# A two-layer hybrid block (gated feed-forward, S5 and sparse attention): the wide GpSimd arithmetic of the S5 preparation and of the rotary products moved to VectorE and ScalarE

## The chip, the cores and the metric

One Trainium2 chip, one NeuronCore of it. The metric is the device time of one execution in microseconds. In the profile PE is TensorE's matmul side and PEld its weight load, DVE is VectorE, ACT is ScalarE, POOL is GpSimd, SP is the SyncE queue that issues the weight transfers.

## What is computed

Input `x` is 256 tokens by 1024, float32. Two layers each do this:

```
x = x + 0.5 * swiglu(rms_norm(x, norm_ffn1), ffn1_wi, ffn1_wo)      # 1024 -> 2*2816 -> 1024
h = rms_norm(x, norm_mix)
u, q, k/v for three attention branches, gates = split(h @ w_in)     # 1024 -> 3864
y_a = s5_branch(u, lambda, dt, b, c, d, w_glu)                      # diagonal state space, 32 groups x 64 states
y_b = nsa_branch(q, k, v, gates, norms, ...) @ nsa_w_up             # rms norm + rotary on q and k, three attentions
x = x + (sigmoid(gate_a) * y_a + sigmoid(gate_b) * y_b) @ w_out
x = x + 0.5 * swiglu(rms_norm(x, norm_ffn2), ffn2_wi, ffn2_wo)
```

The S5 branch needs matrices that depend on parameters alone: powers of a complex decay per state, the scaled input matrix times these powers, the output matrix times these powers, and a short convolution kernel over four lags. The kernel calls this the preparation and does it once per layer. Rotary embedding multiplies each head by a cosine table and its swapped halves by a sine table, and adds the two.

## The kernel before

**Weights and matmuls.** Every matmul is computed as three float32r passes: a weight tile of 128x1024 is loaded by SP into `raw` (four buffers) and split into a rounded part `whi` by ACT and a remainder `wlo` by DVE. Gain-scaled weights (`wi`, `w_in`) are split by lines 156 and 157, in two pieces of 128x512 for each tile; the others (`wo`) by line 318 in one piece of 128x1024. There are four `whi` and four `wlo` buffers, so a tile can be split only when PE is done with the tile four places earlier. Lines 350 to 352 are the three passes.

**A feed-forward network** runs over 11 chunks of 256 hidden columns. In each chunk PE does the gate and up products of this chunk (four weight tiles, 48 matmuls into `gu`), then the output products of the chunk before (two tiles, 24 matmuls into `ya` and `yb`, one for each half of the tokens). ACT applies silu (line 450), DVE multiplies (line 451, result `w1k`), PE transposes the result (line 434), and ACT and DVE split it (line 318, `w1k`). After the last chunk `finish` runs the output products of that chunk, adds `ya` and `yb` to `x` on DVE (line 360), transposes the new `x` on PE (line 344) and splits it into `hh` (ACT) and `hl` (DVE): the stationary operand of every matmul of the next stage. I call this stretch the end of the first feed-forward network.

**The preparation of the S5 parameters** is a generator that runs beside the first feed-forward network of each layer: `prep` calls `s5_load`, `s5_scalars`, `s5_tables` and `s5_mats`. Each `yield` gives back a cost; `next`, which hands out the next weight tile, pulls from the generator until a credit of 0.75 is used up. What is left when the network has been written is written out in one piece by `drain_bg`, before the mixing stage. `cmul` is a complex product: four products and two sums. In `s5_mats` it is called three times for 128x256 operands and four times for 128x512 operands with the four products on POOL (`M=G`), which cost nothing against the credit.

**The rotary products** are in `normrope` (keys, and one compressed key) and `normrope_q`: the cosine product on DVE, the two swapped halves with the sine on POOL, the sum on DVE.

**The order of the instructions** on each engine is set when the kernel is built: a scheduler simulates the program and lists each engine's instructions by simulated time, with the written order as priority. At run time each engine takes its list strictly in order.

Of the kernel before, what the change touches and what calls it, by code (L numbers as in the profile page):

```python
# [74 lines left out]
class Model:  # L75
# [445 lines left out]
            nc.gpsimd.dma_start(P['c'][:, i], bass.AP(tensor=t, offset=o, ap=[[64, 128], [8192, 4], [1, 64]]))  # L521
        k.P = P

    def cmul(k, o, a, b, tmp, cost, M=None, conj=False):

        V = k.nc.vector
        M = M or V
        c = cost if M is V else 0.0
        t0, t1 = tmp(), tmp()
        M.tensor_mul(t0, a[0], b[0])  # L530
        yield c
        M.tensor_mul(t1, a[1], b[1])
        yield c
        (V.tensor_add if conj else V.tensor_sub)(o[0], t0, t1)
        yield cost
        t2, t3 = tmp(), tmp()
        M.tensor_mul(t2, a[0], b[1])
        yield c
        M.tensor_mul(t3, a[1], b[0])
        yield c  # L540
        (V.tensor_sub if conj else V.tensor_add)(o[1], t2, t3)
        yield cost

# [127 lines left out]
    def s5_tables(k):  # L671

        nc, P = k.nc, k.P
        V, G = nc.vector, nc.gpsimd
        cs = k.sb([128, 16, 64], "r4", k.opt['n4'])
        sn = k.sb([128, 16, 64], "r4", k.opt['n4'])
        de = k.sb([128, 16, 64], "r4", k.opt['n4'])
        P['cs'], P['sn'], P['de'] = cs, sn, de
        G.memset(cs[:, :, 0:1], 1.0)
        G.memset(sn[:, :, 0:1], 0.0)  # L680
        k.gcopy(de, P['m4'][:, :, None].to_broadcast([128, 16, 64]))
        G.memset(de[:, :, 0:1], 0.0)
        R = k.sb([128, 14, 16], "w1k", k.opt['n1'])
        cur = P['u4']
        m = 1
        i = 0
        while m < 64:
            W = [k.sb([128, 16, m], "w2k", k.opt['n2']) for _ in range(2)]
            br = cur[0][:, :, None].to_broadcast([128, 16, m])
            bi = cur[1][:, :, None].to_broadcast([128, 16, m])  # L690
            c0, s0 = cs[:, :, 0:m], sn[:, :, 0:m]
            c1, s1 = cs[:, :, m:2 * m], sn[:, :, m:2 * m]
            cost = 0.07 + 0.0167 * m
            V.tensor_mul(W[0], c0, br)
            yield cost
            V.tensor_mul(W[1], s0, bi)
            yield cost
            V.tensor_sub(c1, W[0], W[1])
            yield cost
            V.tensor_mul(W[0], s0, br)  # L700
            yield cost
            V.tensor_mul(W[1], c0, bi)
            yield cost
            V.tensor_add(s1, W[0], W[1])
            yield cost
            m *= 2
            if m < 64:
                nx = (R[:, 2 * i], R[:, 2 * i + 1])
                t0, t1 = R[:, 12], R[:, 13]
                V.tensor_mul(t0, cur[0], cur[0])  # L710
                V.tensor_mul(t1, cur[1], cur[1])
                V.tensor_sub(nx[0], t0, t1)
                V.tensor_mul(t0, cur[0], cur[1])
                V.tensor_scalar(nx[1], t0, 2.0, None, op0=ALU.mult)
                yield 0.4
                cur = nx
                i += 1

    def s5_mats(k):
        nc, P = k.nc, k.P  # L720
        V, G, S = nc.vector, nc.gpsimd, nc.scalar
        r4 = lambda: k.sb([128, 1024], "r4", k.opt['n4'])
        r8 = lambda: k.sb([128, 2048], "r8", k.opt['n8'])
        b, pw, f = P['b'], P['pw'], P['f']
        bc = lambda s, n=16: s[:, :, None].to_broadcast([128, 16, n])
        tmp1 = lambda: k.sb([128, 16, 16], "w1k", k.opt['n1'])

        X = [r4().rearrange("p (a t c) -> p a t c", a=16, t=4) for _ in range(2)]
        bb = (X[0][:, :, 3], X[1][:, :, 3])
        yield from k.cmul(bb, (bc(f[0]), bc(f[1])), (b[:, 0], b[:, 1]), tmp1, 0.34)  # L730
        for m in (1, 2, 3):
            yield from k.cmul((X[0][:, :, 3 - m], X[1][:, :, 3 - m]), (bc(pw[m][0]), bc(pw[m][1])), bb, tmp1, 0.34, G)

        CT = []
        for i in range(2):
            cd = k.sb([128, 4, 2, 64], "w2k", k.opt['n2'])
            V.tensor_mul(cd, P['c'][:, i, :, None].to_broadcast([128, 4, 2, 64]), k.C('m2')[:, None, :, None].to_broadcast([128, 4, 2, 64]))
            bk = k.bank((128, 4, 128))
            for q in range(4):
                nc.tensor.transpose(bk[:, q], cd[:, q].rearrange("p a b -> p (a b)"), k.id)  # L740
            ct = k.sb([128, 16, 32], "w2k", k.opt['n2'])
            S.copy(ct.rearrange("p (q r) c -> p q (r c)", q=4), bk)
            CT.append(ct)
            yield 0.6
        nci = k.sb([128, 16, 32], "w2k", k.opt['n2'])
        V.tensor_scalar(nci, CT[1], -1.0, None, op0=ALU.mult)
        yield 0.34

        P['G'], XX = [], []
        for i in range(2):  # L750
            xx = r8().rearrange("p (a g c) -> p a g c", a=64, g=2)
            for g in range(2):
                G.tensor_scalar(xx[:, :, g], X[i].rearrange("p a t c -> p (a t) c"), k.C('m64')[:, g:g + 1], 0.0,
                                op0=ALU.mult, op1=ALU.add)
            xx = xx.rearrange("p (a t) g c -> p a (t g c)", a=16)
            XX.append(xx)
            gm = r8().rearrange("p (a b) -> p a b", a=16)
            for h in range(4):
                bk = k.bank((128, 4, 128))
                for q in range(4):  # L760
                    nc.tensor.transpose(bk[:, q], xx[:, h * 4 + q], k.id)
                S.copy(gm[:, h * 4:h * 4 + 4], bk)
                yield 0.5
            P['G'].append(gm)

        bk = k.bank((128, 4, 64))
        for q in range(4):
            for i, c in enumerate((CT[0], nci)):
                for r in range(4):
                    p = 4 * q + r  # L770
                    nc.tensor.matmul(bk[r * 32:(r + 1) * 32, q], c[:, p], X[i][:, p].rearrange("p t c -> p (t c)"),
                                     start=(q == 0 and i == 0), stop=(i == 1), skip_group_check=True)
        lt = k.sb([128, 16, 2, 16], "w2k", k.opt['n2'])
        V.tensor_mul(lt, bk.rearrange("p q (t c) -> p (q t) c", t=4)[:, :, None].to_broadcast([128, 16, 2, 16]),
                     k.C('m2')[:, None, :, None].to_broadcast([128, 16, 2, 16]))
        yield 0.6
        lt = lt.rearrange("p (q t) g c -> p q (t g c)", q=4)
        bk = k.bank((128, 4, 128))
        for q in range(4):
            nc.tensor.transpose(bk[:, q], lt[:, q], k.id)  # L780
        bk = bk.rearrange("p q (r c) -> p (q r) c", r=4)
        lag = k.sb([128, 16, 32], "w2k", k.opt['n2'])
        S.copy(lag, bk)
        yield 0.5
        dg = k.sb([128, 16, 32], "w2k", k.opt['n2'])
        V.tensor_mul(dg[96:128], k.C('i32')[96:128, None, :].to_broadcast([32, 16, 32]),
                     P['d'][96:128, :, None].to_broadcast([32, 16, 32]))
        yield 0.6
        V.tensor_add(lag[96:128], lag[96:128], dg[96:128])
        yield 0.6  # L790
        ks = r8().rearrange("p (a s c) -> p a s c", a=16, s=4)
        G.memset(ks, 0.0)
        for t in range(4):
            for s in range(t, 4):
                r = 3 - s + t
                k.gcopy(ks[t * 32:(t + 1) * 32, :, s], lag[r * 32:(r + 1) * 32])
        P['K'] = ks.rearrange("p a s c -> p a (s c)")

        cr, ci = (r8().rearrange("p (a s c) -> p a s c", a=16, s=4) for _ in range(2))
        tmp2 = lambda: k.sb([128, 16, 32], "w2k", k.opt['n2'])  # L800
        for s in range(4):
            a = (bc(pw[s + 1][0], 32), bc(pw[s + 1][1], 32))
            yield from k.cmul((cr[:, :, s], ci[:, :, s]), a, (CT[0], nci), tmp2, 0.6, G, True)
        P['C'] = [m.rearrange("p a s c -> p a (s c)") for m in (cr, ci)]


# [128 lines left out]
    def normrope(k, src, nh, cg, sg, out, tabs):  # L935
# [14 lines left out]
        for h in range(2):  # L950
            a, b = slice(h * 32, h * 32 + 32), slice((1 - h) * 32, (1 - h) * 32 + 32)
            T, Q = tabs(t2), tabs(qn)
            ix = (slice(None),) * (len(T.shape) - 1)
            G.tensor_mul(T[ix + (a,)], Q[ix + (b,)], sg[ix + (a,)])
        V.tensor_add(out, tabs(t1), tabs(t2))

    def kv_evac(k, t, kp, ps):
# [41 lines left out]
    def normrope_q(k, src, cg, sg, out):  # L999
# [11 lines left out]
        V.tensor_mul(t1, qn, cg)  # L1011
        for h in range(2):
            a, b = slice(h * 32, h * 32 + 32), slice((1 - h) * 32, (1 - h) * 32 + 32)
            G.tensor_mul(t2[:, :, a], qn[:, :, b], sg[:, :, a])
        for g in range(2):
            V.tensor_add(out[:, g], t1[:, g * 4:g * 4 + 4], t2[:, g * 4:g * 4 + 4])

# [355 lines left out]
```

## Time and profile before

| | us |
|---|---|
| median of three runs | 1189.49 (1189.47 to 1189.8) |
| the profiled execution | 1189.75 |
| its span, first to last instruction | 1187.7 |
| PE busy | 1157.4 |
| DVE busy | 840.5 |
| ACT busy | 674.7 |
| POOL busy | 232.2 |

The time outside the span is 2.05 us. PE is busy for 97% of the span, so there are about 30 us in which it has nothing to do; of these 7.35 us lie in the first 25 us and 4.1 us behind its last matmul. DVE is busy for 71% of the span on average, and for over 90% in the stretches in which POOL computes.

### The profile page before, as it was taken

The numbers are of one execution on the slowest core, as the hardware profiler recorded it, in microseconds if no ns is written. First come the engines' busy times: TensorE is split into PE (matmuls) and PEld (weight loads), VectorE is DVE, ScalarE is ACT, GpSimd is POOL, SyncE is SP. The second block draws the span as 40 slices with busy tenths as digits, with TensorE's granted clock in tenths as the row PEclk, the third lists the DMA queues.
The fourth block names the chain that finished last, engine by engine and source line by source line (L and its number), as shares of the span: only waits on it lengthen the run. The fifth ranks groups of instructions, "written<-read, shape, count | busy, mean of one in ns | idle before, by whom it ended". The sixth has DMA issues, their size and how long they took to land.

```text
span 1187.7 us, 18769 instructions
## 1 busy us (share of the span) xinstructions
PE 1157.4 (97%) x6710; PEld 944.1 (79%) x6710; DVE 840.5 (71%) x1494; ACT 674.7 (57%) x1176; POOL 232.2 (20%) x284
## 2 busy tenths in 40 slices
PE   7999999999999999999999999999999999999998
PEld 6888777877877888888888887778778778888886
DVE  5797979587976765555567987886878756655554
ACT  6655554755775565555566555546557646655552
POOL 3001644035032000000030044711441310000000
PEclk9999999999999999999999999999999999999999
DMA  7756555365442565655565656445635435656652
GB/s 236 221 182 194 154 157 186 103 184 168 143 142 92 168 213 185 194 182 186 185 193 173 197 165 183 138 156 154 196 108 170 132 105 161 214 181 192 189 183 89
DMA packets 150077, 200.46 MB, mean 169 GB/s; under 512 B 9952, under 2 KB 120832, under 8 KB 149984
## 3 DMA queue, kind: packets, MB, share of 16 engines
q1 hardware_dynamic: 148848, 197.46, 53.8%
q0 software_dynamic: 1136, 1.82, 0.9%
q8 instruction: 52, 0.85, 0.3%
q14 instruction: 41, 0.34, 0.1%
HBM read 198.18 MB, written 1.05 MB: 168 GB/s over the span
## 4 chain that ended last, share of the span: by engine, by line
PE 89%; POOL 3%; DVE 3%; ACT 2%; issue 2%; DMA 1%; SPq 0%; DVEq 0%; ACTq 0%
PE gu L352 19%; PE gu L350 19%; PE gu L351 19%; PE ya L352 4%; PE yb L350 4%; PE ya L350 4%; PE yb L352 4%; PE yb L351 4%; PE ya L351 4%; POOL r L480 2%; PE tr L434 2%; PE yb L1178 1%; DVE wlo L157 1%; PE tr L344 1%; PE tr L1167 1%
## 5 line engine op out<-in xcount | busy, mean ns | idle before, releaser
L157 DVE SCALAR_TENSOR_TENSOR wlo<-raw,gcol,whi 128x512 fp32r<-128x512 f32 (+2 forms) x480 | 359.0, 786 | 111.0 <-ACT whi L156 108.5
L156 ACT ACTIVATE whi<-raw,gcol 128x512 fp32r<-128x512 f32 (+2 forms) x480 | 316.2, 710 | 193.8 <-PE gu L351 91.0
L350 PE MATMUL gu<-whi,hh 128*128 128x512 f32 (+2 forms) x960 | 378.7, 395 | 0.4 <-ACT whi L156 0.4
L352 PE MATMUL gu<-wlo,hh 128*128 128x512 f32 (+2 forms) x960 | 375.4, 396 | 2.5 <-DVE wlo L157 2.5
L351 PE MATMUL gu<-whi,hl 128*128 128x512 f32 (+2 forms) x960 | 375.3, 391 | 0.0
L318 DVE TENSOR_TENSOR wlo<-raw,whi 128x1024 fp32r<-128x1024 f32 x128 | 161.0, 1260 | 102.0 <-ACT whi L318 99.3
L352 PEld LDWEIGHTS gu<-wlo,hh 128*128 128x128 f32 x960 | 180.8, 189 | 38.6 <-DVE wlo L157 2.8
L318 ACT CAST whi<-raw 128x1024 fp32r<-128x1024 f32 x128 | 134.5, 1053 | 133.3 <-PE gu L351 114.8
L351 PEld LDWEIGHTS gu<-whi,hl 128*128 128x128 f32 x960 | 181.2, 189 | 35.7
L350 PEld LDWEIGHTS gu<-whi,hh 128*128 128x128 f32 x960 | 181.3, 189 | 34.7 <-ACT whi L156 0.6
L325 POOL TENSOR_SCALAR rs<-ss 128x1 f32<-128x1 f32 (+3 forms) x22 | 7.2, 328 | 379.4 <-ACT w2k L332 352.6
L351 PE MATMUL yb<-whi,w1k 128*128 128x512 f32 x176 | 71.5, 406 | 0.7 <-DVE w1k L318 0.7
L352 PE MATMUL yb<-wlo,w1k 128*128 128x512 f32 x176 | 69.1, 393 | 0.0
L350 PE MATMUL yb<-whi,w1k 128*128 128x512 f32 x176 | 69.0, 395 | 0.0
L351 PE MATMUL ya<-whi,w1k 128*128 128x512 f32 x176 | 68.8, 391 | 0.0
L352 PE MATMUL ya<-wlo,w1k 128*128 128x512 f32 x176 | 68.7, 390 | 0.0
L350 PE MATMUL ya<-whi,w1k 128*128 128x512 f32 x176 | 68.2, 393 | 0.0
L318 ACT CAST w1k<-tr 128x256 fp32r<-128x256 f32 x88 | 32.5, 369 | 46.1 <-PE tr L434 46.1
L1157 POOL TENSOR_SCALAR w2k<-w2k,sm 128x128 f32<-128x128 f32 (+1 forms) x64 | 38.9, 629 | 99.8 <-ACT w2k L1141 62.8
L451 DVE SCALAR_TENSOR_TENSOR w1k<-gu,rs,w1k 128x256 f32<-128x256 f32 x88 | 42.0, 479 | 20.3 <-ACT w1k L450 20.2
L450 ACT ACTIVATE w1k<-gu,rs 128x256 f32<-128x256 f32 x88 | 40.9, 468 | 22.7 <-PE gu L352 17.8
L318 DVE TENSOR_TENSOR w1k<-tr,w1k 128x256 fp32r<-128x256 f32 x88 | 36.7, 419 | 10.3 <-ACT w1k L318 10.2
(307 smaller groups left out, 1474.7 us busy)
## 6 DMA issues: line engine op xcount, KB each, us to landing
raw<-in_ffn_wi_dram SPq DMA_DIRECT2D x352, 256.0 KB, 3.3
raw<-in_ffn_wo_dram SPq DMA_DIRECT2D x88, 512.0 KB, 3.6
raw<-in_w_in_dram SPq DMA_DIRECT2D x48, 512.0 KB, 4.4
raw<-in_ssm_w_glu_dram SPq DMA_DIRECT2D x32, 256.0 KB, 3.4
raw<-in_w_out_dram SPq DMA_DIRECT2D x16, 512.0 KB, 3.2
raw<-in_cmp_w_dram SPq DMA_DIRECT2D x8, 512.0 KB, 4.6
raw<-in_nsa_w_up_dram SPq DMA_DIRECT2D x16, 256.0 KB, 3.9
raw<-in_w_in_dram SPq DMA_DIRECT2D x8, 408.0 KB, 4.1
```

The source lines that it names most:

```text
L156: k.hi_ins[i] = k.nc.scalar.activation(hi[:, s], r[:, s], AF.Copy, scale=c)
L157: k.nc.vector.scalar_tensor_tensor(lo[:, s], r[:, s], c, hi[:, s].bitcast(F32), op0=ALU.mult, op1=ALU.subtract)
L318: return k.nc.scalar.copy(hi, src), k.nc.vector.tensor_sub(lo, src, hi.bitcast(F32))
L344: m = k.nc.tensor.transpose(b[:, i], src[:, i * 128:(i + 1) * 128], k.id)
L350: mm(ps, a[0], b[0], start=first, stop=False)
L351: mm(ps, a[1], b[0], start=False, stop=False)
L352: return mm(ps, a[0], b[1], start=False, stop=last)
L434: nc.tensor.transpose(b[:, i], act[t][:, i * 128:(i + 1) * 128], k.id)
L450: m = nc.scalar.activation(sg, ps[t][:, :256], AF.Silu, scale=r[t])
L451: nc.vector.scalar_tensor_tensor(a, ps[t][:, 256:], r[t], sg, op0=ALU.mult, op1=ALU.mult)
L480: k.nc.gpsimd.tensor_scalar(o, i, 1.0, 0.0, op0=ALU.mult, op1=ALU.add)
L1157: G.tensor_scalar(w[:, i], p[:, i], cf[:, j:j + 1], 0.0, op0=ALU.mult, op1=ALU.add)
```

## The change

The four products of every `cmul` go to DVE and count against the credit. Of the four wide multiplications that spread `X` over the two group halves in each layer, two go to ACT and two to DVE. The spreading of `m4` goes to ACT. The ten lag copies go to DVE (six) and ACT (four). The six rotary products of the keys and the four of the queries go to DVE. All of these were on POOL, which keeps the norms' small operations, the memsets, its transfers, the copies into `kc2` and the attention weights of line 1157.

```diff
-    def cmul(k, o, a, b, tmp, cost, M=None, conj=False):
+    def cmul(k, o, a, b, tmp, cost, conj=False):
 
         V = k.nc.vector
-        M = M or V
-        c = cost if M is V else 0.0
         t0, t1 = tmp(), tmp()
-        M.tensor_mul(t0, a[0], b[0])
-        yield c
-        M.tensor_mul(t1, a[1], b[1])
-        yield c
+        V.tensor_mul(t0, a[0], b[0])
+        yield cost
+        V.tensor_mul(t1, a[1], b[1])
+        yield cost
         (V.tensor_add if conj else V.tensor_sub)(o[0], t0, t1)
         yield cost
         t2, t3 = tmp(), tmp()
-        M.tensor_mul(t2, a[0], b[1])
-        yield c
-        M.tensor_mul(t3, a[1], b[0])
-        yield c
+        V.tensor_mul(t2, a[0], b[1])
+        yield cost
+        V.tensor_mul(t3, a[1], b[0])
+        yield cost
...
-        k.gcopy(de, P['m4'][:, :, None].to_broadcast([128, 16, 64]))
+        k.nc.scalar.copy(de, P['m4'][:, :, None].to_broadcast([128, 16, 64]))
...
-            yield from k.cmul((X[0][:, :, 3 - m], X[1][:, :, 3 - m]), (bc(pw[m][0]), bc(pw[m][1])), bb, tmp1, 0.34, G)
+            yield from k.cmul((X[0][:, :, 3 - m], X[1][:, :, 3 - m]), (bc(pw[m][0]), bc(pw[m][1])), bb, tmp1, 0.34)
...
-                G.tensor_scalar(xx[:, :, g], X[i].rearrange("p a t c -> p (a t) c"), k.C('m64')[:, g:g + 1], 0.0,
-                                op0=ALU.mult, op1=ALU.add)
+                o, v, w = xx[:, :, g], X[i].rearrange("p a t c -> p (a t) c"), k.C('m64')[:, g:g + 1]
+                if g:
+                    V.tensor_scalar(o, v, w, None, op0=ALU.mult)
+                else:
+                    S.activation(o, v, AF.Copy, scale=w)
+                yield 1.2
...
-                k.gcopy(ks[t * 32:(t + 1) * 32, :, s], lag[r * 32:(r + 1) * 32])
+                (S.copy if (s + t) % 2 else V.tensor_copy)(ks[t * 32:(t + 1) * 32, :, s], lag[r * 32:(r + 1) * 32])
+                yield 0.3
...
-            yield from k.cmul((cr[:, :, s], ci[:, :, s]), a, (CT[0], nci), tmp2, 0.6, G, True)
+            yield from k.cmul((cr[:, :, s], ci[:, :, s]), a, (CT[0], nci), tmp2, 0.6, True)
...
-            G.tensor_mul(T[ix + (a,)], Q[ix + (b,)], sg[ix + (a,)])
+            V.tensor_mul(T[ix + (a,)], Q[ix + (b,)], sg[ix + (a,)])
...
-            G.tensor_mul(t2[:, :, a], qn[:, :, b], sg[:, :, a])
+            V.tensor_mul(t2[:, :, a], qn[:, :, b], sg[:, :, a])
```

In the changed file the lines of `cmul` are 528, 530, 535 and 537 for the products and 532 and 539 for the sums, and the lag copies are line 798.

**First place: DVE's list at the end of the first feed-forward network.** Before, between the two silu products (`w1k<-gu,rs`) of the last chunk and the two additions to the first token half of `x`, the list holds weight splits and the splits of the transposed activations alone:

```order
L318 TENSOR_TENSOR wlo<-raw,whi 128x1024 x3
L451 SCALAR_TENSOR_TENSOR w1k<-gu,rs,w1k 128x256
L318 TENSOR_TENSOR wlo<-raw,whi 128x1024
L451 SCALAR_TENSOR_TENSOR w1k<-gu,rs,w1k 128x256
L157 SCALAR_TENSOR_TENSOR wlo<-raw,gcol,whi 128x512 x2
L318 TENSOR_TENSOR w1k<-tr,w1k 128x256
L157 SCALAR_TENSOR_TENSOR wlo<-raw,gcol,whi 128x512 x2
L318 TENSOR_TENSOR w1k<-tr,w1k 128x256
L360 SCALAR_TENSOR_TENSOR x<-ya,x 128x512 x2
```

Now the same stretch, from the split of the first activation half to the second addition, reads as follows (`w2k` are the temporaries of `cmul`, `r_2077` and `r_2078` its results):

```order
L318 TENSOR_TENSOR w1k<-tr,w1k 128x256
L532 TENSOR_TENSOR r_2077<-w2k 128x16x32
L535 TENSOR_TENSOR w2k<-s5q,w2k 128x512
L537 TENSOR_TENSOR w2k<-s5q,w2k 128x512
L528 TENSOR_TENSOR w2k<-s5q,w2k 128x512
L530 TENSOR_TENSOR w2k<-s5q,w2k 128x512
L535 TENSOR_TENSOR w2k<-s5q,w2k 128x512
L537 TENSOR_TENSOR w2k<-s5q,w2k 128x512
L360 SCALAR_TENSOR_TENSOR x<-ya,x 128x512
L539 TENSOR_TENSOR r_2078<-w2k 128x16x32
L532 TENSOR_TENSOR r_2077<-w2k 128x16x32
L360 SCALAR_TENSOR_TENSOR x<-ya,x 128x512
```

Nine instructions of 128x512 from `cmul` now stand between the activation's last split and the second addition, and 14 more, with six lag copies and two operations of 32x512, stand ahead of them among the weight splits of the last chunk. The list of the second layer is the same.

**Second place: PE's list at the same end.** Before, the eight transposes of `x` stand between the last output product of the first token half and the first of the second half:

```order
L351 MATMUL ya<-whi,w1k 128x512
L352 MATMUL ya<-wlo,w1k 128x512
L344 MATMUL tr<-id,x 128x128 x8
L350 MATMUL yb<-whi,w1k 128x512
L351 MATMUL yb<-whi,w1k 128x512
```

Now one matmul of the next stage stands between the two groups of four transposes, and nothing else:

```order
L351 MATMUL ya<-whi,w1k 128x512
L352 MATMUL ya<-wlo,w1k 128x512
L344 MATMUL tr<-id,x 128x128 x4
L350 MATMUL gu<-whi,hh 128x512
L344 MATMUL tr<-id,x 128x128 x4
L350 MATMUL yb<-whi,w1k 128x512
```

The twelve `yb` matmuls still stand behind both groups, so PE can't start them before DVE has added both halves of the first 128 tokens.

**Third place: the norm and rotary products of the compressed key.** Before, POOL's list has the reciprocal roots (325, 326), then the key's two sine products (`nr_2772`), then those of the queries:

```order
L325 TENSOR_SCALAR rs<-ss_2764 32x1
L326 TENSOR_TENSOR rs<-rs,mh 32x1
L325 TENSOR_SCALAR rs<-ss_2894 128x8
L326 TENSOR_TENSOR rs<-rs,mh 128x8
L954 TENSOR_TENSOR nr_2772<-nr_2769,cc 32x32 x2
L1014 TENSOR_TENSOR w2k<-w2k,sg 128x8x32 x2
```

Now DVE's list has the key's products right behind its norm, and the copy `kb` that PE transposes follows two places later:

```order
L950 TENSOR_TENSOR nr_2769<-tr,rs 32x64
L952 TENSOR_TENSOR nr_2771<-nr_2769,cc 32x64
L957 TENSOR_TENSOR nr_2772<-nr_2769,cc 32x32 x2
L318 TENSOR_TENSOR kT<-tr,kT 64x2x128
L958 TENSOR_TENSOR kc<-nr_2771,nr_2772 32x64
L157 SCALAR_TENSOR_TENSOR wlo<-raw,gcol,whi 128x512
L1049 COPY kb<-kc 32x128
```

The key's chain no longer passes through POOL behind the queries' reciprocal root.

## Rows read from the trace of the kernel before

**Rows 1.** The head of the page: span, and busy time of each engine.
```profile
span 1187.7 us, 18769 instructions
PE 1157.4 (97%) x6710; PEld 944.1 (79%) x6710; DVE 840.5 (71%) x1494; ACT 674.7 (57%) x1176; POOL 232.2 (20%) x284
```
**Rows 2.** PE's waits over the whole span: total us, times, longest.
```profile
PE tr L1053 <- DVE kb L1046: 3.3, 2, 1.6
...
PE tr L434 <- DVE w1k L451: 2.9, 2, 1.4
PE tr L761 <- DVE w1k L318: 2.9, 2, 1.4
...
PE yb L351 <- DVE w1k L318: 0.7, 2, 0.3
```
**Rows 3.** PE's timeline: start, duration, instruction, idle time before it and its releaser.
```profile
189.26 0.44 PE L434 MATMUL tr<-id,w1k 128*128 128x128 f32 x2 [1.45 <-DVE w1k L451]
...
288.35 0.22 PE L1053 MATMUL tr<-id,kb 32*128 32x32 f32 x1 [1.62 <-DVE kb L1046]
```
**Rows 4.** Windows in the second layer: busy us (count); the last three: clock, DMA, GB/s.
```profile
872.00:876.00 4.00, 2.60 (x10) 2.16 (x11) 3.37 (x7) 2.77 (x6) 3.83 (x1) 0.84 0.72 208
876.00:880.00 4.00, 4.00 (x14) 3.16 (x14) 2.59 (x6) 0.00 (x0) 1.24 (x2) 0.73 0.79 221
```
**Rows 5.** Timelines of POOL and of DVE around 183 us.
```profile
182.39 1.50 POOL L532 TENSOR_TENSOR w2k<-s5q,w2k 128x512 f32<-128x512 f32 x1
...
182.90 1.53 DVE L157 SCALAR_TENSOR_TENSOR wlo<-raw,gcol,whi 128x512 fp32r<-128x512 f32 x1
```
**Rows 6.** DVE's timeline where POOL is idle, two pieces.
```profile
71.86 0.75 DVE L157 SCALAR_TENSOR_TENSOR wlo<-raw,gcol,whi 128x512 fp32r<-128x512 f32 x1
72.52 0.22 DVE L696 TENSOR_TENSOR w2k<-r,w1k 128x64 f32<-128x64 f32 x1
...
82.98 0.68 DVE L694 TENSOR_TENSOR w2k<-r,w1k 128x512 f32<-128x512 f32 x1
83.58 1.22 DVE L318 TENSOR_TENSOR wlo<-raw,whi 128x1024 fp32r<-128x1024 f32 x1
84.72 0.42 DVE L704 TENSOR_TENSOR r<-w2k 128x256 f32<-128x256 f32 x1
85.05 0.17 DVE L714 TENSOR_SCALAR w1k<-w1k 128x16 f32<-128x16 f32 x1
```
**Rows 7.** DVE's groups by line and form: count, busy us, mean ns of one.
```profile
L789 DVE TENSOR_TENSOR w2k<-w2k 32x512 f32<-32x512 f32 x1 | 0.7, 689 | 0.0
...
L820 DVE COPY r<-r 32x256 f32<-32x256 f32 x8 | 3.0, 381 | 4.0 <-ACT r L1225 3.9
```
**Rows 8.** DVE's timeline at the end of the first feed-forward network, layer 1.
```profile
196.29 3.48 DVE L318 TENSOR_TENSOR wlo<-raw,whi 128x1024 fp32r<-128x1024 f32 x3
199.70 0.47 DVE L451 SCALAR_TENSOR_TENSOR w1k<-gu,rs,w1k 128x256 f32<-128x256 f32 x1
200.93 1.23 DVE L318 TENSOR_TENSOR wlo<-raw,whi 128x1024 fp32r<-128x1024 f32 x1 [0.76 <-ACT whi L318]
...
203.60 1.42 DVE L157 SCALAR_TENSOR_TENSOR wlo<-raw,gcol,whi 128x512 fp32r<-128x512 f32 x2 [1.05 <-ACT whi L156]
...
207.27 1.50 DVE L360 SCALAR_TENSOR_TENSOR x<-ya,x 128x512 f32<-128x512 f32 x2
```
**Rows 9.** ACT's timeline: one cast of an output weight tile.
```profile
193.64 1.05 ACT L318 CAST whi<-raw 128x1024 fp32r<-128x1024 f32 x1 [1.69 <-PE gu L351]
```
**Rows 10.** PE's timeline at the same end: its first and last steps.
```profile
199.17 0.39 PE L350 MATMUL ya<-whi,w1k 128*128 128x512 f32 x1
...
208.82 0.66 PE L344 MATMUL tr<-id,x 128*128 128x128 f32 x4 [0.16 <-DVE x L360]
209.24 0.47 PE L350 MATMUL yb<-whi,w1k 128*128 128x512 f32 x1
...
212.08 0.39 PE L350 MATMUL gu<-whi,hh 128*128 128x512 f32 x1
```

## The prediction

> **What bounds the kernel now.** I read the page's head first. PE is busy for 1157.4 of 1187.7 us [rows 1], so the time is PE's work plus its waits, and a gain for DVE, ACT or POOL counts only where PE waits for it. PE takes its list in order, so a late result delays everything behind it. Next come PE's waits. Those that name DVE's chains are short: 2.9 us for the silu product, 2.9 for the split of an activation, 0.7 for the same at `yb`, 3.3 for `kb`, two of each kind, one in each layer [rows 2]. Their places are in PE's timeline [rows 3]: the silu product at 189.26 us, beside POOL's `cmul` products, and `kb` behind the queries' reciprocal root on POOL. Together they are 9.8 us.
>
> After the `kb` wait of the second layer the windows show PE at a granted clock of 0.84 and then 0.73 for 4 us each [rows 4], between its levels of 2.4 and 1.2 GHz: (0.16 + 0.27) x 4 = 1.7 us lost behind a wait of 1.6 us. By the Trainium skill, "TensorE: Matmul & The Clock Gate", section "Why this matters for your kernels", idle gaps between matmul bursts drop the clock to half; the trace agrees in direction, and if only the wait itself counted this term would be nothing.
>
> POOL's products also stretch what DVE does beside them: a 128x512 product takes POOL 1.50 us, and a `wlo` split of the same width takes DVE 1.53 us next to it [rows 5] against 0.75 where POOL is idle [rows 6].
>
> **Prices.** On DVE consecutive instructions overlap a little, so I take the distance from start to start [rows 6]: 83.58 - 82.98 = 0.60 us for a product of 128x512, 0.33 for 128x256, 0.66 for a `wlo` split of 128x512, 1.14 for one of 128x1024. A sum of 128x512 has the same operand sizes as the product and gets 0.60. The two operations on 32x512 get 0.60 each (one alone shows 0.69 with its tail [rows 7]). A lag copy on DVE, 32 partitions by 512 out of a strided place, is not in the trace: from 0.33 (a plain operation of 256) to 0.60 (of 512) is the bound, 0.45 my value, because the nearest row, a strided copy of half the size, takes 0.38 [rows 7].
>
> **A: what is removed.** All four waits come from POOL's products or from POOL's place in the key's chain, so I let all 9.8 us go, and the clock's 1.7 us: -11.5. The other bound is 0, if the same instructions wait for something else.
>
> **The chunks in the middle.** One chunk of PE is 72 matmuls at 0.237 us (twelve in 2.84 us, between 209.24 and 212.08 [rows 10]), 17 us. DVE's own share is four tiles of `wi` at 2 x 0.66, two of `wo` at 1.14, two silu products at 0.47 [rows 8] and two activation splits at 0.33: 9.2 us. The preparation's credit puts 5 to 6.5 us beside it. That is 14 to 16 us, so DVE keeps up, and the largest block between two splits, 4 to 5 us, is covered by the tiles already split, at 12 matmuls or 2.84 us each. I take 0 here. If that cover is gone, each chunk costs what DVE exceeds it by; a rival prices that.
>
> **B: what is added, at the end of the first network.** This decides. The products of the output matrix come last in the preparation, and the order puts 23 products and sums, six lag copies and two 32x512 operations between the split of the second `wo` tile of the last chunk but one (written with PE's output products one chunk later) and the second addition to `x`. Before, these were on POOL, or placed in an earlier chunk. The addition can't be passed: DVE's list is in order, PE's transposes of `x` need both additions, and the `yb` products and the next stage stand behind the transposes.
>
> DVE's own work in this stretch: three `wo` splits 3.42, two silu products 0.94, four `wi` pieces 2.64, two activation splits 0.66, two additions 1.50 [rows 6, 8]: 9.16 us. Added: 23 x 0.60 + 2 x 0.60 + 6 x 0.45 = 17.7. Together 26.9 us without a gap.
>
> When can it start? The first of these `wo` splits needs a weight buffer, which PE frees when 24 matmuls and 4 transposes of the chunk are still to come, 24 x 0.237 + 0.42 = 6.1 us before its output products begin; ACT's cast of 1.05 us comes first [rows 9]. So DVE starts about 5.0 us before the first `ya` product, at 199.17 in before [rows 10]. The second addition ends 26.9 - 5.0 = 21.9 us after it. Four transposes (0.42, 208.82 to 209.24) and twelve `yb` products (2.84) follow, and the next stage's `gu` starts 25.1 us after the first `ya`. Before, that is 212.08 - 199.17 = 12.9 us [rows 10]. The difference is 12.2 us a layer. It would show as three new waits of PE: about 1 us for the second silu product, 5 for the activation's split, the rest for the additions. The second layer has the same list: +24.4, with the copy's bounds 22.8 to 26.
>
> **C: the clock behind them.** The new waits are longer than the one that lowered the clock in [rows 4]. I charge that row's 1.7 us once for each layer: +3.4. The bounds are 0 and twice that.
>
> **Elsewhere.** In the mixing stage DVE gets, in each layer, four small key products of 0.2 to 0.33 and four query products of 0.33, some 2 us in a stretch in which it waits for PE much of the time; ACT gets a copy and two spreads of 1024 columns (1.05 each, as its cast [rows 9]) and four lag copies, under 6 us against the 43% of the span in which it is idle [rows 1]. I cost both at 0. If ACT's cover failed its casts would be late, and the splits behind them, by at most one such instruction, about 1 us.
>
> **Sum.** The profiled execution took 1189.75 us: its span and 2.05 us outside. 1189.75 - 11.5 + 24.4 + 3.4 = 1206.05. The median of the runs lies 0.26 below the profiled one, so 1205.8. With all of A, the lower B and no C it is 1201; with half of A, the upper B and twice C, 1217.
>
> **Rivals.**
> 1. *The list is drained before PE comes.* Then only A counts: 1189.49 - 11.5 = 1178. For it: DVE is busy for 71% on average [rows 1], it had 5.4 us free in this very stretch (199.17 - 5.0 to 207.27 + 1.50 is 14.6 us [rows 8, 10], less its own 9.16), and without POOL beside it each split takes half as long. Against: the stretch starts with a split that waits for PE's buffer, so earlier idle time is no use to it. It decides if 12 us or more of the 17.7 run ahead of that split or are cheaper than I price them. By the Trainium skill, "GPSIMD Engine Reference", section "4.1 Engine selection", two-input elementwise work belongs on VectorE, GpSimd being about half as fast; that rule speaks for this rival, and [rows 5, 6] agree (1.50 against 0.60 us). Chance 0.11.
> 2. *The two cancel.* The end costs about 5.7 us a layer, because the split is freed earlier or the additions slip forward: 1189.5, within 0.2%. Chance 0.04.
> 3. *DVE becomes the bound of the middle chunks too.* If instructions follow each other at their full durations (0.75, 1.23, 0.68) and not at these distances, a chunk needs about 1.5 us more than PE gives in the four chunks of each layer that carry the most preparation: 2 x 4 x 1.5 = 12 us more, 1217.5. For it: [rows 5] show how easily DVE is stretched. Against: with POOL quiet, [rows 6] show the short distances. Chance 0.12.
>
> **How the numbers follow.** My forecast, 1205.8, has 0.73. The start of the stretch is the softest term: 2 us either way in each layer is 4 us, which puts the low end at 1197 with A's share; the high end, 1220, takes in rival 3. Rivals 1 and 2 (0.15) and a little of the ends are left out. 0.2% is 2.4 us, about what a measurement of this kernel can tell from no change. Faster 0.11, same 0.04, slower 0.85.
>
> **What would show it.** Right, step by step: the waits for `kb` and for the silu product beside POOL are gone; POOL's busy time falls by more than half; at the end of the first network, in both layers, PE waits for the silu product, the activation's split and the additions, 10 us or more a layer, while DVE is busy without a gap from about 190 to 220 us; the clock is below 1 there. Wrong: the output products follow one another at the end of the network as before (rival 1); PE waits for `wlo` in every chunk of the second half (rival 3); or the clock stays at 1 behind the new waits, which takes C away.

## The result

The changed kernel takes 1215.28 us (median of four runs, 1212.55 to 1216.73), before 1189.64: the ratio is 1.0217, with a 95% interval of 1.0205 to 1.0229. It is 25.6 us slower; the prediction was 1205.8, with a range of 1197 to 1220. The profiled execution took 1215.75 us.

### The profile page after: what moved, and what is told of

It is laid out like the page before. It is cut to its first block, busy times and chain, and to the rows that moved or that the text cites. A ratio compares the mean times of both kernels' runs of the same rounds, so it can differ in the third digit from the quotient of the medians.

```text
span 1214.0 us, 18754 instructions
## 1 busy us (share of the span) xinstructions
PE 1167.6 (96%) x6710; PEld 951.8 (78%) x6710; DVE 831.3 (68%) x1586; ACT 686.1 (57%) x1190; POOL 88.6 (7%) x178
## 4 chain that ended last, share of the span: by engine, by line
PE 90%; DVE 5%; ACT 3%; issue 1%; DMA 1%; SPq 0%; DVEq 0%; ACTq 0%
PE gu L352 20%; PE gu L350 20%; PE gu L351 19%; PE yb L350 4%; PE yb L351 4%; PE yb L352 4%; PE ya L352 4%; PE ya L350 4%; PE ya L351 4%; PE tr L434 2%; PE yb L1181 1%; PE tr L344 1%; PE tr L1170 1%; PE ya L1137 1%; PE yb L856 1%
## 5 line engine op out<-in xcount | busy, mean ns | idle before, releaser
L157 DVE SCALAR_TENSOR_TENSOR wlo<-raw,gcol,whi 128x512 fp32r<-128x512 f32 (+2 forms) x480 | 335.2, 739 | 138.1 <-ACT whi L156 135.7
L318 DVE TENSOR_TENSOR wlo<-raw,whi 128x1024 fp32r<-128x1024 f32 x128 | 156.5, 1224 | 108.7 <-ACT whi L318 107.8
L351 PE MATMUL ya<-whi,w1k 128*128 128x512 f32 x176 | 70.6, 401 | 9.8 <-DVE w1k L318 9.8
L350 PE MATMUL ya<-whi,w1k 128*128 128x512 f32 x176 | 70.1, 402 | 2.5 <-ACT w1k L318 2.5
L351 PEld LDWEIGHTS ya<-whi,w1k 128*128 128x128 f32 x176 | 34.1, 194 | 17.5 <-DVE w1k L318 10.3
```

Of the source, the lines that this page charges most:

```text
L157: k.nc.vector.scalar_tensor_tensor(lo[:, s], r[:, s], c, hi[:, s].bitcast(F32), op0=ALU.mult, op1=ALU.subtract)
L318: return k.nc.scalar.copy(hi, src), k.nc.vector.tensor_sub(lo, src, hi.bitcast(F32))
L350: mm(ps, a[0], b[0], start=first, stop=False)
L351: mm(ps, a[1], b[0], start=False, stop=False)
```

## The profile after

The page's head answers to [rows 1]: POOL's busy time has fallen from 232 to 89 us, and the span has grown by 26.3 us, while PE's share has hardly moved. That a long wait is there can't be seen in it.

```profile
span 1214.0 us, 18754 instructions
PE 1167.6 (96%) x6710; PEld 951.8 (78%) x6710; DVE 831.3 (68%) x1586; ACT 686.1 (57%) x1190; POOL 88.6 (7%) x178
```

PE's waits (total us, times, longest) answer to [rows 2]. The waits for `kb` and for the split before the transposes of `r` are gone. In their place stand, in each layer, a chain at the end of the first network (`w1k` twice on DVE, `x`, and twice ACT) and two waits for ACT in the mixing stage, L1265 and L1172.

```profile
PE ya L351 <- DVE w1k L318: 9.8, 2, 4.9
...
PE gu L350 <- ACT r L1265: 3.2, 4, 1.4
PE tr L434 <- DVE w1k L451: 3.1, 2, 1.6
PE tr L1170 <- ACT w2k L1172: 2.7, 2, 1.4
...
PE tr L344 <- DVE x L360: 2.6, 2, 1.5
PE ya L350 <- ACT w1k L318: 2.5, 2, 1.2
...
PE gu L350 <- ACT hh L318: 1.4, 2, 0.7
```

DVE's timeline at the end of the first network of layer 1 answers to [rows 8]. The first row is the split with which the stretch begins, the last the second addition to `x`. No idle time over 0.1 us lies between them; nearly every row between is a product, a sum or a split of its usual length, and the six lag copies take 0.43 us each.

```profile
189.33 1.23 DVE L318 TENSOR_TENSOR wlo<-raw,whi 128x1024 fp32r<-128x1024 f32 x1 [0.72 <-ACT whi L318]
190.59 0.69 DVE L788 TENSOR_TENSOR w2k<-cst,s5q 32x512 f32<-32x512 f32 x1
191.31 0.69 DVE L528 TENSOR_TENSOR w2k<-s5q,w2k 128x512 f32<-128x512 f32 x1
...
213.92 0.68 DVE L360 SCALAR_TENSOR_TENSOR x<-ya,x 128x512 f32<-128x512 f32 x1
214.52 0.68 DVE L539 TENSOR_TENSOR r<-w2k 128x512 f32<-128x512 f32 x1
215.12 0.68 DVE L532 TENSOR_TENSOR r<-w2k 128x512 f32<-128x512 f32 x1
215.72 0.68 DVE L360 SCALAR_TENSOR_TENSOR x<-ya,x 128x512 f32<-128x512 f32 x1
```

PE's timeline answers to [rows 10] down to 222.21 us, and then to [rows 3]. From the first `ya` (194.24) to the end of the second addition (216.40) it is 22.16 us, against 208.77 - 199.17 = 9.60 before [rows 8, 10]. The rest up to the next stage's second `gu` matmul (222.21) is 5.81 us, against 3.54 before (to 212.31). The twelve `yb` matmuls take 4.46 us, not 2.84. Further on, `kb` is there in time (295.82), but 2 us later PE waits for ACT; and the scores of the last attention unit (376.72) stand behind the last weight matmul.

```profile
194.24 0.39 PE L350 MATMUL ya<-whi,w1k 128*128 128x512 f32 x1
...
203.62 0.41 PE L434 MATMUL tr<-id,w1k 128*128 128x128 f32 x2 [1.57 <-DVE w1k L451]
208.91 0.80 PE L351 MATMUL ya<-whi,w1k 128*128 128x512 f32 x1 [4.89 <-DVE w1k L318]
...
214.66 1.12 PE L344 MATMUL tr<-id,x 128*128 128x128 f32 x4 [1.11 <-DVE x L360]
...
217.75 0.78 PE L350 MATMUL yb<-whi,w1k 128*128 128x512 f32 x1
...
222.21 0.39 PE L351 MATMUL gu<-whi,hl 128*128 128x512 f32 x1
...
295.82 0.24 PE L1056 MATMUL tr<-id,kb 32*128 32x32 f32 x1
...
297.85 0.50 PE L350 MATMUL gu<-whi,hh 128*128 128x512 f32 x1 [1.41 <-ACT r L1265]
...
376.49 0.39 PE L352 MATMUL gu<-wlo,r 128*128 128x512 f32 x1
376.72 0.62 PE L1137 MATMUL ya<-kT,qT 128*128 128x512 f32 x2
...
381.10 0.63 PE L1170 MATMUL tr<-id,w2k 128*128 128x128 f32 x4 [1.36 <-ACT w2k L1172]
...
388.15 0.66 PE L344 MATMUL tr<-id,r 128*128 128x128 f32 x4
```

Two places of the kernel before, in PE's timeline: the second `gu` matmul of the next stage, to which the 3.54 us run, and the end of the attention. There the last scores are issued at 360.54, 8.8 us ahead of the end of the weight matmuls, so softmax runs beside these.

```profile
212.31 0.39 PE L351 MATMUL gu<-whi,hl 128*128 128x512 f32 x1
...
360.54 1.09 PE L1134 MATMUL ya<-kT,qT 128*128 128x512 f32 x4
...
368.90 0.39 PE L352 MATMUL gu<-wlo,r 128*128 128x512 f32 x1
...
375.06 0.66 PE L344 MATMUL tr<-id,r 128*128 128x128 f32 x4
```

The windows (the last three columns are clock, DMA share and GB/s) answer to [rows 4]: PE waits 1.2 and 1.6 us, and as the long wait begins the granted clock falls to its lower level, where it is from 204 to 220 us; it falls again behind the wait of 1.4 us in the second layer.

```profile
204.00:208.00 4.00, 0.02 (x1) 0.00 (x0) 4.00 (x8) 0.37 (x1) 0.00 (x0) 0.53 0.68 173
208.00:212.00 4.00, 3.09 (x7) 2.48 (x8) 4.00 (x8) 0.00 (x0) 0.00 (x0) 0.50 0.52 155
...
216.00:220.00 4.00, 3.55 (x10) 2.92 (x11) 2.29 (x4) 0.98 (x2) 0.00 (x0) 0.50 0.02 4
...
896.00:900.00 4.00, 4.00 (x12) 3.14 (x13) 3.97 (x9) 1.22 (x2) 0.00 (x0) 0.64 0.80 247
```

To see where the 26.3 us of the span lie, I compared the distances between the same PE instructions in one trace of each kernel. The first network runs up to the first `ya` product of S5 (L488); "to `kb`" from there to the transpose of `kb`; the attention from there to the first transpose of the gated sum (`tr<-id,r`, 375.06 and 388.15). In us longer than before, layer 1 / layer 2; the last column is the median against the kernel before on the same chip:

| | first network | to `kb` | attention | time |
|---|---|---|---|---|
| changed | 10.3 / 9.9 | -2.4 / -2.4 | 5.6 / 5.8 | +25.6 |
| e1 query products on POOL | 10.4 / 10.0 | -2.1 / -2.4 | 1.5 / 1.2 | +19.0 |
| e2 key products on POOL | 8.2 / 9.7 | -0.2 / -0.2 | 3.4 / 1.6 | +23.7 |
| e3 credit 1.0 | 7.6 / 3.2 | -2.4 / -1.7 | 4.4 / 4.1 | +16.6 |
| e4 = e3 and e1 | 8.4 / 3.2 | -2.1 / -2.4 | 1.8 / 1.3 | +10.5 |
| e5 before, query products on DVE | -2.0 / 0.0 | -0.2 / -0.2 | 3.1 / 1.7 | +3.7 |
| e6 PE kept busy | 8.4 / 9.7 | -2.4 / -2.4 | 10.6 / 2.3 | +26.0 |
| e7 output matrix behind the end | 7.7 / 10.6 | -3.3 / -3.6 | 5.8 / 2.8 | +23.3 |
| e8 = e7 and e1 | 7.8 / 9.7 | -3.1 / -2.1 | 3.1 / 1.3 | +16.4 |
| e9 output matrix among the transposes | -4.6 / -2.7 | -2.4 / -2.4 | 3.1 / 2.7 | -5.6 |
| e10 the same, credit 0.75 | 3.6 / 5.2 | -1.4 / -0.4 | 1.9 / 2.7 | +12.1 |
| e11 without the output matrix | -3.7 / -2.1 | -2.4 / -2.4 | 6.4 / 8.2 | +1.9 |

Three things in the columns can't be put down to the edits. From PE's first instruction to its twenty-first `gu` matmul the trace of the kernel before takes 13.0 us and the others 11.1 to 12.9, with the same PE list there; by this the first figure of the first column comes out too low (by 0.7 for the changed kernel, 1.8 for e5, 1.9 for e9, 1.6 for e11). In the attention PE has in every trace a wait without a releaser in the profile, 1.0 us in the kernel before and up to 2.7 in e11, mostly in the second layer. And in the second layer the kernel before lost 1.7 us to the clock [rows 4], which some of the other traces lose and some don't. The traces of e7 and e11 are also not those of a median run: 2.8 us under it and 2.6 us over it. That of e5 has 1.4 us more than the others behind its last matmul.

## The experiments

After the result I held two theories. Theory E: the end of the first network is long because DVE's list holds the output matrix there (it gives 20 of the 26 us). Theory Q: the query products on DVE reorder the attention, which gives the 11.4 us in the attention that the prediction had costed at nothing. The rivals were that the attention is late for other reasons (L, or K for the key products), and that DVE is short in the middle chunks as well (M).

**e1_query_pool**

```diff
-            V.tensor_mul(t2[:, :, a], qn[:, :, b], sg[:, :, a])
+            G.tensor_mul(t2[:, :, a], qn[:, :, b], sg[:, :, a])
```

> The change with one part undone: the four query sine products are on POOL again, everything else as changed. Theory Q (the query products on DVE change the order in which PE gets the attention units, so that the last units run behind the last weight matmul, 5.6 to 5.8 us a layer): these 11.4 us come back, about 1204 us, and PE's list ends the attention as before. Rival L (attention ends later because the whole layer starts it later, or because DVE is busier): at most the products' own 2 us, 1213 or more.

1208.06 us, ratio 1.0157 (1.0142 to 1.0172), 7.2 us less than the changed kernel, or 6.6 when each is taken against the kernel before on its own chip. Rival L falls: the attention shrinks by 4.1 and 4.7 us, and PE's list has the order of before again, with the last scores 8.8 us ahead of the end of the weight matmuls (at 379.05). PE's timeline of this run:

```profile
370.29 1.08 PE L1137 MATMUL ya<-kT,qT 128*128 128x512 f32 x4
...
378.66 0.39 PE L352 MATMUL gu<-wlo,r 128*128 128x512 f32 x1
...
384.81 0.66 PE L344 MATMUL tr<-id,r 128*128 128x128 f32 x4
```

From the last weight matmul to the gated sum it is 5.76 us here and 5.77 before, but 11.3 in both layers of the changed kernel. The gain is less than the 11.4 us that I had expected. The 1.5 us that stay in layer 1 are the waits for L1265 (1.41 and 0.24). They are there in layer 2 too, but there the clock stays at 1, which is worth 1.7 us against the kernel before.

**e2_key_pool**

```diff
-            V.tensor_mul(T[ix + (a,)], Q[ix + (b,)], sg[ix + (a,)])
+            G.tensor_mul(T[ix + (a,)], Q[ix + (b,)], sg[ix + (a,)])
```

> The change with another part undone: the key sine products are on POOL again, the query products stay on DVE. Theory Q: the stretch of the attention stays as long as in the changed kernel, and the wait for the compressed key's copy comes back (1.6 us a layer, with some clock): 1217 to 1220 us. Rival K (the key products moved the attention): about 11 us less, 1204.

1212.73 us, ratio 1.0204 (1.0187 to 1.0221): neither. The wait for `kb` is back (1.40 us) and costs nothing, since the L1265 wait is gone with it. In layer 1 the stretch from S5 to the end of the attention is 3.2 us longer than before in this kernel (-0.2 + 3.4) and in the changed one (-2.4 + 5.6). In layer 2 it is 1.4 us here (-0.2 + 1.6) and 3.4 in the changed kernel, whose clock falls behind the L1265 wait there, while here it stays at 1. The attention's order is that of the changed kernel, as theory Q says. PE's timeline of this run:

```profile
296.32 0.21 PE L1056 MATMUL tr<-id,kb 32*128 32x32 f32 x1 [1.40 <-DVE kb L1049]
...
296.73 0.50 PE L350 MATMUL gu<-whi,hh 128*128 128x512 f32 x1
```

Why one takes the other's place is seen in ACT's timelines, first of the kernel before, then of the changed one. The tanh that frees the `gu` bank stands behind eight weight casts in both.

```profile
282.41 5.50 ACT L156 ACTIVATE whi<-raw,gcol 128x512 fp32r<-128x512 f32 x8 [1.42 <-PE gu L351]
287.82 0.67 ACT L1262 ACTIVATE r<-gu,rh 128x512 f32<-128x512 f32 x1
```

```profile
291.85 5.23 ACT L156 ACTIVATE whi<-raw,gcol 128x512 fp32r<-128x512 f32 x8
297.10 0.69 ACT L1265 ACTIVATE r<-gu,rh 128x512 f32<-128x512 f32 x1
```

Before, the tanh ended at 288.49, and PE, held up by `kb` until 288.35 [rows 3], came to that bank right afterwards. Take the first wait away, and PE stands 1.4 us in front of the second.

**e3_credit and e4_credit_query_pool**

```diff
-BG=0.75
+BG=1.0
```

(e4 has e1's edit as well.)

> The changed kernel with one number changed: the credit of the preparation is 1.0 instead of 0.75 a weight tile, so all products of the output matrix stand in chunks before the last. Theory E (the end of the first network costs 14 to 15 us a layer because DVE's list holds 17.7 us more there, and because of the clock behind that wait): both terms go, 1215.3 - 28.7 = 1186.6 us, and the clock stays at 1. Rival M (DVE is short in the middle chunks as well): PE waits for weight remainders there and gives back up to 12 us: about 1198.

> Credit 1.0 and the query products on POOL, the rest as changed. Theories E and Q together, if their terms are independent: 1215.3 - 28.7 - 11.4 = 1175 us, 14 us under the kernel before, which is what the waits that the change removes are worth. If either theory is only a share of the truth: 1180 to 1190.

1205.60 us (1.0138, 1.0121 to 1.0155) and 1199.51 us (1.0082, 1.0065 to 1.0099). Both are longer than theory E gave, in e4 together with Q (1186.6 and 1175), and than the rivals beside it did. The end of the first network is as short as before (9.57 us from the first `ya` to the second addition), but the first network is still 7.6 and 3.2 us longer in all: rival M holds a share. The 24 instructions now stand in blocks of up to five, with the lag copies among them, between splits of two chunks in the middle, and PE waits there in both layers, with the granted clock at 0.50 from 172 to 176 us. In layer 1 it also waits 3.6 us at 62 us, where DVE's list is full of the preparation's small operations: the credit packs the whole preparation closer, so e3 isn't a test of the output matrix alone. PE's timeline of e3:

```profile
173.44 0.79 PE L351 MATMUL yb<-whi,w1k 128*128 128x512 f32 x1 [4.16 <-DVE w1k L318]
```

The query products are worth 6.1 us between these two.

**e5_before_query_dve.** The kernel before, with this edit alone:

```diff
-            G.tensor_mul(t2[:, :, a], qn[:, :, b], sg[:, :, a])
+            V.tensor_mul(t2[:, :, a], qn[:, :, b], sg[:, :, a])
```

> The kernel before with one part of the change alone: the four query sine products on DVE. Theory Q (they alone reorder the attention units on PE): the stretch from the compressed key's copy to the end of the attention grows by 4.1 to 4.7 us a layer, as it fell when they were put back: 1189 + 8.5 = about 1197.5 us, with the rest of the program as before. Rival (the reordering needs the other parts too, or only follows from the later start): within 2 us of 1189.

1192.81 us, ratio 1.0035 (1.0022 to 1.0048): the query products alone make the kernel slower, by 3.7 us, not by 8.5. In layer 1 the tail behind the last weight matmul is again 11.28 us for 5.77, but that matmul ends 2.5 us earlier after `kb` (78.48 for 80.94 us), since small attention work has moved behind it. In layer 2 the attention is only 1.7 us longer, but there the clock stays at 1 behind the `kb` wait, where the kernel before lost 1.7 us. So about 3 us a layer is what the order costs by itself. In the changed kernel's attention the L1265 wait comes on top, in place of the `kb` wait ahead of it.

**e6_pe_busy**

```diff
         def part(t, i0):
+            if t == 0 and hooks:
+                d = k.bank((128, 512), 'gu')
+                for j in range(32):
+                    k.nc.tensor.matmul(d, aT[last, 0][0][:, 0], Ws[0][0][:, :512], start=j == 0, stop=j == 31)
```

> The changed kernel with 32 more matmuls (128x512, on operands that are there already, result not read) in PE's list of each layer, in the place where PE waits for the last activation split at the end of the first network. Theory C (the clock that falls behind that wait costs 1.5 to 2.5 us a layer): the granted clock stays at 1 there, PE's waits become matmuls, and 3 to 5 us come back: 1211 us. Rival (the lower clock is hidden, since DVE's list sets the end): 1215, or more where the added matmuls run past the wait.

1215.06 us, ratio 1.0219 (1.0204 to 1.0235): nothing came back in all. In layer 1 the clock stayed at 1 until 214 us, and the first network was 2.0 us shorter than in the changed kernel. But PE then waited 2.8 us for the additions and the clock fell behind this wait instead; in layer 2 the gain was 0.2. The attention of layer 1 is 5.0 us longer than in the changed kernel: the clock fell twice more (0.60 and 0.64 in a window), and PE's wait without a releaser is here, with 2.6 us; that of layer 2 has neither and is 3.5 us shorter. So this run moved the clock's cost and doesn't give its size.

**e7_c_behind and e8_c_behind_query_pool**

```diff
+        def cmat():
...
+                for _ in range(6):
+                    with k.tc.issue_after(k.pin.ins):
+                        c = next(g)
+                    yield c
...
+        k.bg, k.budget = k.cmat, 1.2
         ps = k.gemm(k.hstat, 8, 512, k.turns(k.opt['O2']))
```

(`pin` is the last split of the transposed `x`; e8 has e1's edit as well.)

> The changed kernel with the 24 products and sums of the output matrix moved behind the last activation split of the first network in DVE's list (into the first gemms of the mixing stage); same engine, same work. Theory E: the 12.2 us and the clock's part at the end of each first network go; what remains there is DVE's lag copies and two small operations, which fit into its free 5.4 us. The first network then gains its removed waits (3 us a layer against before). The query products' 4.5 us a layer stay, and the new place may cost up to 4 us a layer where 12 us of products stand ahead of a weight split: 1189 - 6 + 9 - 2 = 1190 us, up to 1198. Rival (the end is long for another reason, the lag copies or ACT's): above 1205.

> As the run before, with the query sine products on POOL again. If theories E and Q are independent, 8.5 us less than that run: 1181 to 1189 us, under the kernel before.

1212.33 us (1.0203, 1.0182 to 1.0223) and 1205.48 us (1.0138, 1.0123 to 1.0154). Both expectations failed. The transposes of `x` start 3.2 us earlier than before in layer 1, so the end of the network is short, with the lag copies still in it. But the stretch behind it, up to S5, is 10.9 us longer. PE's waits of e7 name it:

```profile
PE tr L1236 <- ACT w2k L1233: 15.7, 4, 4.3
```

Theory E holds for the end itself (11.28 us from the first `ya` to the second addition), but the new place costs nearly as much. PE waits twice a layer for the copy of `u` on ACT; ahead of it in ACT's list are casts that waited for weight buffers, and the norm's squares. That DVE's six products ahead of the splits of `w_in` started this is likely from the order and not shown. The query products are worth 6.9 us between the two, with some 3 us either way, as e7's four runs spread from 1209.5 to 1214.7.

**e9_c_among_g85 and e10_c_among_g75**

```diff
                 S.copy(gm[:, h * 4:h * 4 + 4], bk)
                 yield 0.5
+                yield from itertools.islice(cm, 3)
```

(`cm` yields the same 24 instructions at a cost of 0.3; both have e1's edit; e9 has BG=0.85.)

> Query products on POOL, and the 24 products and sums of the output matrix on DVE as in the change, but written three at a time behind each transposed group of the input matrix (chunks 7 to 9 of the first network, where the changed kernel's DVE is idle for 18 of 40 us), with a credit of 0.85. Theory E, as the runs so far leave it: these 14 us of DVE cost time only where DVE has no idle time to take them. Then the first network is 2 to 3.2 us a layer shorter than before, the mixing stage about 1 us, and the time is 1181 to 1185 us. Rival M (DVE has no room in the middle chunks, or PE waits behind each block): 1189 or more.

> The same with the credit left at 0.75, which spreads the products over one chunk more and leaves the matrix of lags for the start of the mixing stage. Theory E: as the run before or 1 to 2 us less, since the early chunks are not filled up: 1180 to 1184 us. Rival: the lag matrix, now late, is waited for in the mixing stage, 1189 or more.

e9 takes 1183.24 us, ratio 0.9954 (0.9941 to 0.9966): faster than the kernel before by 5.6 us, as expected. The first network is 4.6 and 2.7 us shorter than before (2.7 in both layers without the difference at the start), although DVE does all the `cmul` products that POOL did. Of PE's waits, those at the end are small:

```profile
PE gu L351 <- ACT r L1272: 3.9, 6, 1.7
...
PE ya L352 <- DVE w1k L319: 1.7, 2, 0.8
...
PE tr L345 <- DVE x L361: 0.7, 2, 0.3
```

In the windows of the changed kernel DVE (third column) is busy for 10.56 and 11.03 of 20 us from 140 to 180 us; in e9 for 19.67 in the first of them, and PE has no wait there. First the changed kernel, then e9:

```profile
140.00:160.00 20.00, 20.00 (x100) 16.53 (x99) 10.56 (x16) 12.64 (x21) 0.00 (x0) 1.00 0.63 191
160.00:180.00 20.00, 20.00 (x97) 16.34 (x96) 11.03 (x17) 10.98 (x18) 0.00 (x0) 1.00 0.56 172
```

```profile
140.00:160.00 20.00, 20.00 (x95) 16.50 (x95) 19.67 (x37) 11.00 (x18) 0.00 (x0) 1.00 0.65 196
```

e10 takes 1200.98 us (1.0102, 1.0087 to 1.0118), the rival's side: at the lower credit the lag matrix falls into the mixing stage, and its copies stand in ACT's list ahead of the copy of `u`, for which PE waits 6.2 us a layer:

```profile
222.29 2.50 ACT L809 COPY r<-w2k 32x512 f32<-32x512 f32 x4
224.81 1.12 ACT L157 ACTIVATE whi<-raw,gcol 128x384 fp32r<-128x384 f32 x2
225.83 1.24 ACT L1231 ACTIVATE w2k<-gu,rs 128x512 f32<-128x512 f32 x2
```

**e11_no_c**

```diff
-        for s in range(4):
-            a = (bc(pw[s + 1][0], 32), bc(pw[s + 1][1], 32))
-            yield from k.cmul((cr[:, :, s], ci[:, :, s]), a, (CT[0], nci), tmp2, 0.6, True)
+        G.memset(cr, 0.0)
+        G.memset(ci, 0.0)
```

> The changed kernel without the 24 products and sums of the output matrix: the matrix is set to zero by two memsets on POOL instead, so this part of the computation is left out. Nothing else is moved. Theory E (they alone make the end of the first network long): the first network is 3.2 us a layer shorter than before, the mixing stage 3.3 us a layer longer as in the changed kernel: 1189 us. Rival (lag copies, ACT's copies or the spreads have a part in it): above 1195.

1190.76 us, ratio 1.0017 (1.0008 to 1.0026). Theory E holds: the first network falls from 10.3 and 9.9 us over before to 3.7 and 2.1 below it, with lag copies, ACT's copies and spreads all in place. The 24 instructions of each layer cost 26 us there in all (25 without the difference at the start), for 48 x 0.60 = 28.8 us of DVE time. From the first `ya` to the end of the second addition it is 11.29 us in layer 1, so that of the 12.56 us more in the changed kernel 1.7 are not theirs; DVE has idle time there again. PE's timeline of this run, then DVE's:

```profile
193.78 0.39 PE L350 MATMUL ya<-whi,w1k 128*128 128x512 f32 x1
```

```profile
204.38 0.69 DVE L360 SCALAR_TENSOR_TENSOR x<-ya,x 128x512 f32<-128x512 f32 x1 [0.47 <-PE ya L352]
```

The attention is 6.4 and 8.2 us longer than before in this trace, more than in the changed kernel: the clock falls behind the L1265 wait in both layers, and in layer 2 again behind the wait of 2.7 us without a releaser.

## Why the prediction was right, and where it was wrong

**B, the end of the first network: right.** Predicted: DVE's list of 26.9 us starts 5.0 us before the first `ya`, the second addition ends 21.9 us after it, 12.2 us a layer more. Measured: 216.40 - 189.33 = 27.07 us, 4.9 us before, 22.16 us after it, 12.56 us more in both layers. The three waits are there with 1.6, 4.9 and 1.1 us. The last was to hold "the rest", some 6 us, and doesn't: the ten `ya` matmuls ahead of it run at the lower clock, 0.43 us apart for 0.23, and PE waits 1.2 and 0.7 us for ACT as well, which the prediction had not. In all PE waits 9.5 us in layer 1, a little under the 10 that were to show. e11 shows that the 24 instructions make 10.9 of the 12.56 us. The bounds were added up a little low: six copies at 0.33 to 0.60 us give 23.0 to 26.2, not 22.8 to 26.

**C, the clock: right in size, by rows alone.** From the second addition to the next stage it is 2.3 us longer in layer 1 and 1.2 in layer 2, together 3.5 against the 3.4 predicted; 1.6 and 1.0 of it are the `yb` matmuls at the lower level, the rest was not split up. That it came so near is in part luck, as 1.7 us was the price of another place. The test with a busy PE was inconclusive. By the Trainium skill, "TensorE: Matmul & The Clock Gate", section "Why this matters for your kernels", idle gaps between matmul bursts drop the clock to half; the 0.50 of the windows from 208 to 220 us, in and behind the wait of 4.9 us, agrees.

**A in the first network: right, a little small.** 1.45 + 1.45 + 0.35 us a layer were to go. Up to the first `ya` the changed kernel is 4.5 and 3.9 us ahead; 0.7 of the 4.5 is the shorter start. With POOL quiet the splits of 128x512 run at 0.73 to 0.76 us throughout. By the Trainium skill, "SBUF — State Buffer", section "Who interferes with whom", DVE and GpSimd share a port pair; the 1.53 us beside POOL [rows 5] and the 0.73 to 0.76 without agree.

**A in the mixing stage: the first step that failed.** "All four waits come from POOL's products or from POOL's place in the key's chain, so I let all 9.8 us go" was wrong for the 3.3 us of `kb` and for the clock. The wait did come from POOL's place in the chain, but ACT's tanh covered it: 1.41 + 0.21 us a layer of new wait took the place of 1.62. The prediction never asked what is late next there, and e2 shows in layer 1 that the exchange is worth nothing. The clock's 1.7 us didn't come back either: in layer 2 it falls to 0.64 behind the new wait.

**"Elsewhere ... I cost both at 0": the second step that failed, and the larger one.** The query products were costed by DVE's busy time. Their price lies in PE's list: with them on DVE the scheduler puts the attention units later among the weight matmuls, and 5.5 us more of the last unit run with no weight matmul beside them. e1, e4 and e8 bring back 6.1 to 6.9 us when the products return to POOL, and e5 loses 3.7 with them alone. That it is the order and not late data is seen at the second query tile: DVE has its sum at 311.41 us, PE transposes it at 315.72 without having been idle. No run has the products on DVE with PE's old order, so the engine's own share isn't measured apart, and why the scheduler's simulation places the units later wasn't followed further. (The keys have six sine products a layer, not four; e2 shows that they don't set the order.)

**The sum.** Predicted: -6.5 (A in the first networks) + 24.4 + 3.4 - 5.0 (`kb` and its clock) = +16.3. Measured: -8.4 + 25.1 + 3.5 + 6.6 = 26.8, and 0.6 less at the start and the end. The miss of 10 us is the mixing stage, which was expected 5.0 shorter and came out 6.6 longer; the larger A made up 1.9 of these 11.6. That the range held the time is luck: its upper sum, 1217, stood for half of A, the upper B and twice C, and the 1220 for rival 3, and none of these is what happened.

**The rivals.** Rival 1, the list drained earlier, is not what the changed kernel does. But it is what e9 makes of it: with the output matrix in the chunks where DVE was idle, 5.6 us are gained and not 25.6 lost. Rival 3 doesn't hold in the changed kernel, as PE has no wait in the middle chunks; it holds in e3, where the same work comes in closer blocks.

## What to carry to other kernels

Price work that is moved to another engine by its place in that engine's list, not by the engine's average load: the 24 products and sums of each layer cost some 25 us in the two layers at the end of a stage, and in e9, with them two chunks earlier, the first network is 2.7 us a layer shorter than before. When a wait is taken away, look in the same timeline for what the waiting engine would meet next and when that is ready. Where a scheduler makes the lists, compare the lists of all engines, PE's above all, also for parts of the change that look too small to matter.

## What the runs showed of the hardware

The granted clock doesn't answer to a wait of 1.4 us in one way: behind the same wait for L1265 it stayed at 1 in layer 1 of the changed kernel and fell to its lower level in layer 2 (0.64 as the mean of 896 to 900 us), and in e6 it fell in layer 1 too (0.60 as the mean of 296 to 300 us). Filling a wait with matmuls (e6) kept it at 1 there, and it fell behind the next wait of 2.8 us. On DVE back-to-back products of 128x512 kept to 0.60 us from start to start over the whole stretch of 27 us.
